# Hybrid decoder layer: the attention's keys and values prepared in the projection stage, and one reciprocal for the gates

## The chip, the core and the metric

One core of a Trainium2 chip runs the whole kernel. Its engines are TensorE (PE), VectorE (DVE), ScalarE (ACT), GpSimd (POOL) and SyncE (SP), each with its own instruction queue that it works off in order; SP only issues transfers here. The metric is the device time of one execution in microseconds; less is better.

## What is computed

A decoder layer on 1024 tokens of width 1024, in float32. One input projection feeds three parts: RWKV-7 time mixing (8 heads), a sparse attention with 8 query heads, 2 groups of keys and values and three branches (compressed, selected, sliding window), and two merge gates. Then come an output projection, cross-attention into 256 memory tokens, and a gated feed-forward net with a convolution. The change concerns the attention's keys and values and its gates:

```python
kv = p[..., NSA_DIM:NSA_DIM + 6 * NSA_KV_DIM].reshape(B, S, 6, G, dh)
k_c, v_c, k_s, v_s, k_w, v_w = [kv[:, :, i] for i in range(6)]
gates = jax.nn.sigmoid(p[..., NSA_DIM + 6 * NSA_KV_DIM:].reshape(B, S, Hq, 3))
q = partial_rope(q, pos)
k_c, k_s, k_w = partial_rope(k_c, pos), partial_rope(k_s, pos), partial_rope(k_w, pos)
...
s_s = jnp.einsum('bgrqd,bgqnkd->bgrqnk', qblk, ks)
p_s = jax.nn.softmax(s_s, axis=-1)
o_s = jnp.einsum('bgrqnk,bgqnkd->bgrqd', p_s, vs)
...
o = jnp.stack([o_c, o_s, o_w], axis=-1)
return jnp.einsum('bshdc,bshc->bshd', o, gates).reshape(B, S, NSA_DIM)
```

The rope turns the first 16 of the 64 numbers of each query and key by an angle that depends on the token.

## The kernel before

Every large float32 product is made of three matmuls in a reduced format (`mm3`, L194 to L197): each operand is split into a high part (a rounding copy, on ACT, L200) and a low part (the rest, a subtraction on VectorE, L201); this pair is `split`. Weights come in pieces by `wload` (L211): SP loads a piece into `raw` (L224; there are two such buffers), and `split` makes `wh` and `wl` of it (two buffers of each in each of two pools).

The program has a first stage (0 to about 210 us) with projections and everything that depends on them alone, the RWKV stage (to about 717 us), the attention stage, and then merge, output projection, cross-attention and feed-forward net. The order of each engine's instructions is fixed when the program is built.

`nsa_proj(cc, n, ...)` (L340) projects all 1024 tokens, in 8 tiles of 128, on n columns that belong to the sparse attention: 24 matmuls for each tile (`np`), an eviction to `nst` by ACT (L347), the rope of the key columns in place by POOL (L355 to L358, once for each z of nb blocks of columns; 128 tokens lie on the partitions), and a store of the tile to `rawn` in DRAM (L359). It is called with cc = 512 and 512 columns (compressed keys and values and the first pair of plain keys and values), with cc = 1024 and 280 columns (the second pair and the gates' 24 columns), and with cc = 0 (queries). The first two calls are called the first and the second projection here. In the first, the first four tiles are worked on together, so that they are complete after 96 matmuls; the other four follow one by one. Between the two lie the key and value projections of the memory (`mk`, `mv`) and transposes of the memory (`mT`); behind the second follow the compression of the keys (`cm`, on blocks `blkh` and `blkl` that are gathered from `rawn`), and more of `mk` and `mv`.

At the start of the attention stage the keys are read back from `rawn` (`kld`, POOL's queue), transposed by PE (`kT`, L985), and copied to `KHt` twice (each half of the partitions holds the high parts, L988, L989), with the low parts in `KL` (L990). The values are read back (`vld`) and split into `VV`. Gate matmuls (`gt`, the merge gates' projection) stand between these on PE. Then blocks of 128 queries follow: `queries(qb)` loads `qr` (L1009) and the gates `gr` (L1011), transposes the queries (`qT`, L1019), and the scores (`sc`, `st`), weights and values follow. `combined` divides by the sum of the weights, which is column 64 of the products, and multiplies by the gate.

Of the kernel before, what the change touches and what calls it, by code (L numbers as in the profile page):

```python
# [126 lines left out]
def layer_kernel(ctx: ExitStack, tc, I, out, cst):  # L127
# [3 lines left out]
    drp = ctx.enter_context(tc.tile_pool(name="drp", bufs=1, space=DRAM))  # L131
# [41 lines left out]
    def pst(name="pst"):  # L173
        return bank("t", name)
# [24 lines left out]
    def split(src, h, l):  # L199
        S.activation(h, src, AF.Copy)  # L200
        V.tensor_sub(l, src, h.bitcast(F32))  # L201
# [33 lines left out]
    def gemmN(o, act, tt, w, cc, n, nk=8):  # L235
        for k in range(nk):
            mm3(o, *act.sta(k, tt), *w.at(k, cc, n), k == 0, k == nk - 1)
# [15 lines left out]
    ps = pst("zz")  # L253
# [26 lines left out]
    wkv = W(2)  # L280
# [29 lines left out]
    for gi, grp in enumerate(groups):  # L310
        n = sum(r for _, r in grp)
        rows = p0.tile([P, P], F32, name=f"rows{gi}")
        o = 0
# [18 lines left out]
    yb = drp.tile([512, T], F32, name="yb")  # L332
    gscr = drp.tile([2048, T], F32, name="gscr")
    rawn = drp.tile([T, NSA_COLS], F32, name="rawn")


    cso = p0.tile([P, 2 * P], F32, name="cso")
    SP.dma_start(cso, cst[:, C_COS:C_CAU])

    def nsa_proj(cc, n, scale, nb, nh, w=None, ahead=lambda tt: None):  # L340
        w = w or wload([win[:, NSA0 + cc:NSA0 + cc + n]])
        for tt in range(NT):
            ahead(tt)
            ps = pg("np")
            gemmN(ps[:, :n], xT, tt, w, 0, n)
            t = stt([P, HALF], name="nst")
            S.activation(t[:, :n], ps[:, :n], AF.Copy, scale=scale)  # L347
            v = t[:, 0:256 * nb].rearrange("p (b h d) -> p b h d", h=4, d=64)[:, :, 0:nh, 0:16]
            for z in range(nb):
                vz = v[:, z]  # L350
                co = cso[:, tt * 16:tt * 16 + 16]
                si = cso[:, P + tt * 16:P + tt * 16 + 16]
                a = p0.tile([P, nh, 16], F32, name="rpa", tag="rpa", bufs=2)
                b = p0.tile([P, nh, 16], F32, name="rpb", tag="rpb", bufs=2)
                G.tensor_tensor(a, vz, bc(co, nh), op=OP.mult)  # L355
                G.tensor_tensor(b[:, :, 0:8], vz[:, :, 8:16], bc(si[:, 0:8], nh), op=OP.mult)
                G.tensor_tensor(b[:, :, 8:16], vz[:, :, 0:8], bc(si[:, 8:16], nh), op=OP.mult)
                G.tensor_tensor(vz, a, b, op=OP.add)  # L358
            SP.dma_start(rawn[tt * P:(tt + 1) * P, cc:cc + n], t[:, :n])  # L359

    rows_h = [slice(0, 64), slice(64, 128)]

# [109 lines left out]
            for u in range(2 * kh, 2 * kh + 2):  # L472
                wkv_split(u)

    nsa_proj(512, 512, 1.0, 2, 2, wkv, first)
    mem_load()
    for rows, pos, n in rowt:
        pt = pst("pv")
# [13 lines left out]
    mem_k(0)  # L492
    mem_v(0)
    blocks = windows(512, "nsa_pe_k")
    nsa_proj(1024, 280, 1.0, 1, 2)
    compress(*blocks, "nsa_ck_w1", "nsa_ck_w2", True)
    mem_k(1)
    blocks_v = windows(640, "nsa_pe_v")
# [451 lines left out]
    with tc.manual_schedule(engines={mybir.EngineType.PE}):  # L950
        while not all(t.done for t in outputs_):
            for tasks in classes:
                t = next((t for t in tasks if not t.done), None)
# [9 lines left out]
    n_scope, npl = opened("npl")  # L963
# [5 lines left out]
    flags = npl.tile([P, 4], F32, name="flags")  # L969
# [2 lines left out]


    gate_chunk(GT)
    KHs, VVs = [], []
    KL = npl.tile([67, 2, 2, T], F32R, name="KL")
    for br, cc in enumerate((768, 1024)):
        kl_ = b8([P, NT, P], name="kld")
        G.dma_start(kl_, rawn[:, cc:cc + P].rearrange("(a p) c -> p a c", p=P))
        KHt = npl.tile([P, 2, T], F32R, name=f"KHt{br}")  # L980
        V.tensor_copy(KL[64:67, br].rearrange("p g t -> p (g t)"), flags[64:67, 2 + br:3 + br].to_broadcast([3, 2 * T]))
        for j in range(2):
            ps = pst("kT")
            for i in range(4):
                PE.transpose(ps[:, i * P:(i + 1) * P], kl_[:, 4 * j + i, :], ident)  # L985
            sl = slice(j * HALF, (j + 1) * HALF)
            for g, rw in enumerate(rows_h):
                S.activation(KHt[rw, g, sl], ps[rw], AF.Copy)  # L988
                S.activation(KHt[rows_h[1 - g], g, sl], ps[rw], AF.Copy)  # L989
                V.tensor_sub(KL[0:64, br, g, sl], ps[rw], KHt[rw, g, sl].bitcast(F32))  # L990
        KHs.append(KHt)
        vl_ = b8([P, NT, 2, 64], name="vld")
        G.dma_start(vl_.rearrange("p a g d -> p a (g d)"), rawn[:, cc + P:cc + 2 * P].rearrange("(a p) c -> p a c", p=P))
        VV = npl.tile([P, NT, 2, 129], F32R, name=f"VV{br}")
        V.memset(VV[:, :, :, 64:65].bitcast(F32), 1.0)
        split(vl_, VV[:, :, :, 0:64], VV[:, :, :, 65:129])
        VVs.append(VV)

    for j in range(2):
        n = (C_ANY - C_CAU) // 2  # L1000
# [4 lines left out]
    def queries(qb):  # L1005
        qr = stt([P, 4, 2, 64], name="qr")
        src = rawn[qb * P:(qb + 1) * P, 0:512].rearrange("t (g r d) -> g t r d", g=2, r=4)
        for g in range(2):
            SP.dma_start(qr[:, :, g, :], src[g])  # L1009
        gr = sm.tile([P, 8, 3], F32, name="gr", tag="gr", bufs=3)  # L1010
        SP.dma_start(gr, rawn[qb * P:(qb + 1) * P, 1280:1304].rearrange("t (h c) -> t h c", c=3))  # L1011
        S.activation(gr, gr, AF.Exp, scale=-1.0)
        V.tensor_scalar(gr, gr, 1.0, None, op0=OP.add)
        V.reciprocal(gr, gr)
        if qb == 0:
            V.tensor_scalar(gr[:, :, 0], gr[:, :, 0], flags[:, 0:1], None, op0=OP.mult)
        ps = pst("qT").rearrange("p (r t) -> p r t", t=P)
        for r in range(4):
            PE.transpose(ps[:, r, :], qr[:, r].rearrange("p g d -> p (g d)"), ident)  # L1019
        Q = npl.tile([P, 8, P], F32R, tag="q", bufs=2, name="Q")  # L1020
        Q2 = b8([67, 2, 4, P], F32R, name="Q2")
        for g, rw in enumerate(rows_h):
            gs = slice(g * 4, g * 4 + 4)
            S.activation(Q[rw, gs, :], ps[rw], AF.Copy)
            V.tensor_sub(Q[rows_h[1 - g], gs, :], ps[rw], Q[rw, gs, :].bitcast(F32))
            S.activation(Q2[0:64, g], ps[rw], AF.Copy)
        return Q, Q2, gr
# [107 lines left out]
    def combined(qb, g, br, t, gr, O):  # L1135

        ps = pst("poT")[:, 0:260].rearrange("p (r n) -> p r n", n=65)
        for r in range(4):
            PE.transpose(ps[:, r, :], t[:, r * P:(r + 1) * P], ident[0:65, 0:65])
        rs = sm.tile([P, 4], F32, name="prs", tag="prs", bufs=4)  # L1140
        V.reciprocal(rs, ps[:, :, 64])
        V.tensor_tensor(rs, rs, gr[:, g * 4:g * 4 + 4, br], op=OP.mult)
        d = O[:, g * 4:g * 4 + 4, :]
        first = br == BRANCHES[0]
        o = d if first else npl.tile([P, 4, 64], F32, name="po2", tag="po2", bufs=2)
        V.tensor_tensor(o, ps[:, :, 0:64], rs[:, :, None].to_broadcast([P, 4, 64]), op=OP.mult)
        if not first:
            G.tensor_tensor(d, d, o, op=OP.add)
        if g == 1 and br == BRANCHES[-1]:
            late.append((LS, lambda: stored(qb, O)))  # L1150
# [103 lines left out]
    for i, (qb, g) in enumerate(items):  # L1254
# [4 lines left out]
        nb = sum(span(qb, br)[1] for br in BRANCHES)  # L1259
# [24 lines left out]
    w = dict(zip((2, 3), cur["wmb"]))  # L1284
# [20 lines left out]
    for j, k in todo:  # L1305
        g = gate_load(1, k, 0, lambda sh, name: stt(sh, name=name))
        ps = pg("mg")
# [117 lines left out]
    for h in range(XQ):  # L1425
        x_query(h)
        if h == 0:
            kvh = [b8([P, 2048], F32R, f"kvh{i}") for i in range(2)]
            kvl = [b8([P, 2048], F32R, f"kvl{i}") for i in range(2)]
            for i in range(2):  # L1430
                t = b8([P, 2048], name="kvld")
# [33 lines left out]
    f = 0  # L1465
    for n in (2, 4, 4, 4, 4, 4):
# [4 lines left out]
        for i in range(n):  # L1471
            w = wload([wup[:, (f + i) * P:(f + i + 1) * P], wup[:, FF + (f + i) * P:FF + (f + i + 1) * P]])
            gt = b8([P, 2, T], F32R, "gT")
            last = [sm.tile([P, 2], F32, name="cl", tag="cl", bufs=6) for _ in range(2)]
            for half in range(2):
                c = []
                for q in range(2):
                    ps = pg("up")
# [4 lines left out]
                hs = slice(half * HALF, (half + 1) * HALF)  # L1483
# [12 lines left out]
        if done:  # L1496
            w = [cols(0), cols(1)]
# [4 lines left out]
        else:  # L1502
            for j in range(2):
                w = cols(j)
# [30 lines left out]
```

## Time and profile before

| | |
|---|---|
| median of 3 runs | 2225.76 us (2222.63 to 2226.09) |
| the profiled execution | 2223.49 us, span 2221.7 us, mean granted PE clock 0.988 |
| PE busy | 2131.7 us, 96% of the span |
| VectorE, ACT, POOL busy | 55%, 40%, 21% |
| transfers | 157.91 MB |

The span is the time from the first to the last instruction that the profile shows; the profiled execution's own time is 1.8 us longer. Busy shares are means over stages with different limits.

### The profile page before, as it was taken

How to read it: one execution, taken by the hardware profiler on the slowest of the kernel's cores; microseconds unless marked ns; L12 is line 12 of the kernel's file. 1: busy time of each engine (PE TensorE's matmuls, PEld its weight loads, DVE VectorE, ACT ScalarE, POOL GpSimd, SP SyncE). 2: the span in 40 equal slices, each digit the busy share in tenths (PEclk: the TensorE clock that was granted, in tenths of full speed). 3: DMA queues.
4: the chain of work that ended last, by engine and by line, in shares of the span. 5: the costliest groups of instructions: out<-in, count | busy, mean ns of one | idle time of the engine just before them, and what ended most of it. 6: DMA issues, size and time to landing. Idle time of an engine off the chain costs nothing.

```text
span 2221.7 us, 31651 instructions
## 1 busy us (share of the span) xinstructions
PE 2131.7 (96%) x12301; PEld 1706.0 (77%) x12301; DVE 1232.4 (55%) x2416; ACT 889.2 (40%) x1441; POOL 475.0 (21%) x544
## 2 busy tenths in 40 slices
PE   9989999999999899999899999999999999999997
PEld 7978777777778667756678877788888888888886
DVE  3422576777652787888656535275444434344447
ACT  3433443544533576776523424142322313132232
POOL 2112231333300244444422101030100101000013
PEclk9999999999999999999999999999999999999999
DMA  6544112121223321112252313111111111111102
GB/s 206 152 150 124 49 24 56 36 52 32 62 59 94 110 66 45 42 45 68 72 189 86 123 38 114 39 39 57 38 48 48 54 42 57 39 57 57 57 29 86
DMA packets 196659, 157.91 MB, mean 71 GB/s; under 512 B 49061, under 2 KB 164766, under 8 KB 196510
## 3 DMA queue, kind: packets, MB, share of 16 engines
q1 hardware_dynamic: 184798, 139.10, 21.2%
q10 hardware_dynamic: 11136, 14.68, 2.0%
q0 software_dynamic: 576, 2.10, 0.3%
q8 instruction: 98, 1.61, 0.3%
q14 instruction: 51, 0.42, 0.1%
HBM read 125.86 MB, written 29.98 MB: 70 GB/s over the span
## 4 chain that ended last, share of the span: by engine, by line
PE 47%; DVE 5%; ACT 2%; DMA 1%; issue 1%; POOL 0%; SPq 0%; ACTq 0%; DVEq 0%; POOLq 0%
PE up L196 7%; PE up L197 7%; PE up L195 7%; PE dn L195 4%; PE dn L197 4%; PE dn L196 4%; PE op L195 2%; PE op L197 1%; PE op L196 1%; PE xq L195 1%; PE xq L196 1%; PE xq L197 1%; DVE acc L1334 1%; ACT acc L1333 1%; DVE bs L1327 1%
## 5 line engine op out<-in xcount | busy, mean ns | idle before, releaser
L200 ACT ACTIVATE wh<-raw 128x1024 fp32r<-128x1024 f32 (+1 forms) x160 | 168.8, 1055 | 474.9 <-PE dn L197 138.1
L201 DVE TENSOR_TENSOR wl<-raw,wh 128x1024 fp32r<-128x1024 f32 (+1 forms) x160 | 198.1, 1239 | 282.5 <-ACT wh L200 281.5
L196 PE MATMUL up<-nTl,wh 128*128 128x512 f32 x704 | 276.5, 393 | 0.0
L197 PE MATMUL up<-nTh,wl 128*128 128x512 f32 x704 | 276.4, 393 | 0.0
L195 PE MATMUL up<-nTh,wh 128*128 128x512 f32 x704 | 276.4, 393 | 0.0
L1458 DVE SCALAR_TENSOR_TENSOR cv<-up,pv,cv 128x511 f32<-128x511 f32 (+1 forms) x176 | 131.5, 747 | 145.4 <-ACT cv L1456 143.4
L1482 POOL TENSOR_TENSOR cv<-cv 128x512 f32<-128x512 f32 x44 | 56.8, 1291 | 630.9 <-DVE cl L1462 413.5
L196 PEld LDWEIGHTS up<-nTl,wh 128*128 128x128 f32 x704 | 132.3, 188 | 29.6
L195 PEld LDWEIGHTS up<-nTh,wh 128*128 128x128 f32 x704 | 132.2, 188 | 29.6
L197 PEld LDWEIGHTS up<-nTh,wl 128*128 128x128 f32 x704 | 132.2, 188 | 29.6
L1106 POOL TENSOR_TENSOR pl<-pe,ph 128x512 fp32r<-128x512 f32 x87 | 114.3, 1317 | 161.3 <-ACT ph L1105 97.3
L195 PE MATMUL dn<-wh,gT 128*128 128x512 f32 x352 | 138.1, 393 | 0.2 <-ACT wh L200 0.2
L197 PE MATMUL dn<-wh,gT 128*128 128x512 f32 x352 | 137.5, 391 | 0.0
L196 PE MATMUL dn<-wl,gT 128*128 128x512 f32 x352 | 136.9, 389 | 0.0
L1493 DVE SCALAR_TENSOR_TENSOR acc<-acc,dn 128x512 f32<-128x512 f32 x96 | 65.5, 686 | 95.5 <-PE dn L197 94.9
L1456 ACT ACTIVATE cv<-up,pv 128x512 f32<-128x512 f32 x88 | 68.5, 778 | 117.2 <-PE up L197 117.2
L195 PE MATMUL gt<-xTh,wh 128*128 128x512 f32 x256 | 113.0, 441 | 0.5 <-DVE nm L1074 0.5
L197 PE MATMUL gt<-xTh,wl 128*128 128x512 f32 x256 | 102.3, 399 | 0.0
L196 PE MATMUL gt<-xTl,wh 128*128 128x512 f32 x256 | 101.9, 398 | 0.0
L1335 POOL TENSOR_TENSOR acc<-acc,lngb 128x1024 f32<-128x1024 f32 x21 | 50.4, 2401 | 206.0 <-DVE acc L1334 129.8
L1105 ACT ACTIVATE ph<-pe 128x512 fp32r<-128x512 f32 (+1 forms) x148 | 90.2, 627 | 6.9 <-POOL macc L1223 4.6
L195 PE MATMUL prj<-xTh,wh 128*128 128x512 f32 x208 | 90.5, 435 | 2.2 <-ACT wh L200 2.2
(365 smaller groups left out, 5092.2 us busy)
## 6 DMA issues: line engine op xcount, KB each, us to landing
raw<-in_ffn_w_up_dram SPq DMA_DIRECT2D x88, 256.0 KB
raw<-in_w_in_dram SPq DMA_DIRECT2D x33, 512.0 KB
raw<-in_ffn_w_down_dram SPq DMA_DIRECT2D x22, 512.0 KB
gscr<-gst ACTq DMA_DIRECT2D x32, 256.0 KB
rawn<-nst SPq DMA_DIRECT2D x16, 256.0 KB
raw<-in_xa_wk_dram SPq DMA_DIRECT2D x8, 512.0 KB
raw<-in_xa_wv_dram SPq DMA_DIRECT2D x8, 512.0 KB
gl<-gscr SPq DMA_DIRECT2D x16, 256.0 KB
```

The costliest lines, as they stand in the source:

```text
L195: PE.matmul(o, lh, rh, start=start, stop=False)
L196: PE.matmul(o, lh, rl, start=False, stop=False)
L197: PE.matmul(o, ll, rh, start=False, stop=stop)
L200: S.activation(h, src, AF.Copy)
L201: V.tensor_sub(l, src, h.bitcast(F32))
L1105: S.activation(h, e, AF.Copy)
L1106: in_turn("l", LTURN)(l, e, h.bitcast(F32), op=OP.subtract)
L1335: (V if tt == NT - 1 else G).tensor_tensor(r[:, c], r[:, c], gb[:, 1, c], op=OP.add)
L1456: S.activation(c, ps, AF.Identity, scale=pc("cw2", ci), bias=pc("ffn_conv_b", ci))
L1458: V.scalar_tensor_tensor(c[:, s:], ps[:, :HALF - s], pc(nme, ci), c[:, s:], op0=OP.mult, op1=OP.add)
L1482: G.tensor_tensor(c[0], c[0], c[1], op=OP.mult)
L1493: V.scalar_tensor_tensor(v, v, 1.0 if f else ALPHA, ps, op0=OP.mult, op1=OP.add)
```

## The change

`nsa_proj` gets an argument `kv = (br, o, keep)` for the first two projections: br is the pair's number (0 or 1), o the first column of its 128 key columns in the tile, and keep the columns that are still stored to `rawn`. For each tile PE transposes the rotated key columns (L370 of the kernel after) into a bank that collects four tiles; after the fourth they are split (`kp`) and stored to DRAM, `KHd` and `KLd`. The value columns are split into `vt`, with a column of ones between, and stored to `VVd`. In the attention stage the transposes, copies, subtractions and value splits are gone; instead `KHt` is loaded from `KHd` by eight transfers of 256 KB, four issued by SP and four by POOL, and `KL` and `VV` by two transfers each on POOL's queue (512 KB and 1032 KB each). The sigmoid 1/(1 + exp(-x)) of a gate and the division by the sum of the weights were two reciprocals, multiplied; now the sum is multiplied by 1 + exp(-x), and one reciprocal is taken. The factor from `flags`, which is 0 for tokens without a compressed block, moves from the gate to that reciprocal.

```diff
-    def nsa_proj(cc, n, scale, nb, nh, w=None, ahead=lambda tt: None):
+    def nsa_proj(cc, n, scale, nb, nh, w=None, ahead=lambda tt: None, kv=None):
...
-            SP.dma_start(rawn[tt * P:(tt + 1) * P, cc:cc + n], t[:, :n])
+            if kv is None:
+                SP.dma_start(rawn[tt * P:(tt + 1) * P, cc:cc + n], t[:, :n])
+                continue
+            br, o, keep = kv
+            SP.dma_start(rawn[tt * P:(tt + 1) * P, cc + keep.start:cc + keep.stop], t[:, keep])
+
+            half, q = divmod(tt, 4)
+            if q == 0:
+                pk = pst("kT")
+            PE.transpose(pk[:, q * P:(q + 1) * P], t[:, o:o + P], ident)
+            if q == 3:
+                kh, kl = (p0.tile([P, HALF], F32R, name="kp", tag=f"kp{i}", bufs=1) for i in range(2))
+                split(pk, kh, kl)
+                hs = slice(half * HALF, (half + 1) * HALF)
+                SP.dma_start(KHd[br][:, hs], kh.bitcast(F32))
+                SP.dma_start(KLd[br][:, hs], kl.bitcast(F32))
+            v = t[:, o + P:o + 2 * P].rearrange("p (g d) -> p g d", g=2)
+            vt = p0.tile([P, 2, 129], F32R, name="vt", tag="vt", bufs=2)
+            V.memset(vt[:, :, 64:65].bitcast(F32), 1.0)
+            split(v, vt[:, :, 0:64], vt[:, :, 65:129])
+            SP.dma_start(VVd[br][tt * P:(tt + 1) * P, :], vt.rearrange("p g c -> p (g c)").bitcast(F32))
...
-    nsa_proj(512, 512, 1.0, 2, 2, wkv, first)
+    nsa_proj(512, 512, 1.0, 2, 2, wkv, first, kv=(0, 256, slice(0, 256)))
...
-    nsa_proj(1024, 280, 1.0, 1, 2)
+    nsa_proj(1024, 280, 1.0, 1, 2, kv=(1, 0, slice(256, 280)))
...
-    for br, cc in enumerate((768, 1024)):
-        kl_ = b8([P, NT, P], name="kld")
-        G.dma_start(kl_, rawn[:, cc:cc + P].rearrange("(a p) c -> p a c", p=P))
...
+    for g, gr_ in enumerate(rows_h):
+        for br in range(2):
+            for e, rw in zip((SP, G), rows_h):
+                e.dma_start(KHs[br][rw, g].bitcast(F32), KHd[br][gr_, :])
+    for br in range(2):
...
-        for j in range(2):
-            ps = pst("kT")
-            for i in range(4):
-                PE.transpose(ps[:, i * P:(i + 1) * P], kl_[:, 4 * j + i, :], ident)
-            sl = slice(j * HALF, (j + 1) * HALF)
-            for g, rw in enumerate(rows_h):
-                S.activation(KHt[rw, g, sl], ps[rw], AF.Copy)
-                S.activation(KHt[rows_h[1 - g], g, sl], ps[rw], AF.Copy)
-                V.tensor_sub(KL[0:64, br, g, sl], ps[rw], KHt[rw, g, sl].bitcast(F32))
...
-        split(vl_, VV[:, :, :, 0:64], VV[:, :, :, 65:129])
-        VVs.append(VV)
+        G.dma_start(KL[0:64, br].bitcast(F32), KLd[br].rearrange("(g d) t -> d g t", g=2))
+        G.dma_start(VVs[br].rearrange("p a g c -> p a (g c)").bitcast(F32), VVd[br].rearrange("(a p) c -> p a c", p=P))
...
-        V.reciprocal(gr, gr)
-        if qb == 0:
-            V.tensor_scalar(gr[:, :, 0], gr[:, :, 0], flags[:, 0:1], None, op0=OP.mult)
...
-        V.reciprocal(rs, ps[:, :, 64])
-        V.tensor_tensor(rs, rs, gr[:, g * 4:g * 4 + 4, br], op=OP.mult)
+        V.tensor_tensor(rs, ps[:, :, 64], gr[:, g * 4:g * 4 + 4, br], op=OP.mult)
+        V.reciprocal(rs, rs)
+        if qb == 0 and br == 0:
+            V.tensor_scalar(rs, rs, flags[:, 0:1], None, op0=OP.mult)
```

**Where the instructions stand.** PE in the first projection, at the end of its first four tiles (96 matmuls). Before, matmul follows matmul:

```order
L195 MATMUL np<-wh,xTh_93 128x512
L196 MATMUL np<-wl,xTh_93 128x512
L197 MATMUL np<-wh,xTl_95 128x512
L195 MATMUL np<-wh,xTh_96 128x512
L196 MATMUL np<-wl,xTh_96 128x512
L197 MATMUL np<-wh,xTl_98 128x512
```

After:

```order
L197 MATMUL np<-wh,xTl_95 128x512
L370 MATMUL kT<-ident,nst 128x128
L195 MATMUL np<-wh,xTh_96 128x512
L370 MATMUL kT<-ident,nst 128x128 x2
L196 MATMUL np<-wl,xTh_96 128x512
L197 MATMUL np<-wh,xTl_98 128x512
L195 MATMUL np<-wh,xTh_96 128x512
L370 MATMUL kT<-ident,nst 128x128
L196 MATMUL np<-wl,xTh_96 128x512
```

The transposes of tiles 0 to 3 stand behind matmuls 96, 97, 97 and 100. Those of tiles 4 to 6 stand five matmuls behind the end of their tile, that of tile 7 behind the end of the projection, three transposes of parameters and six of `mT`. In the second projection they stand behind matmuls 39 and 54, then every 24 (six behind the end of their tile), and the last one eight `cm` matmuls behind the end. Each waits for ACT and POOL.

SP at the start of the attention stage, before:

```order
L224 DMA raw<-in_w_in_dram 128x8x128
L970 DMA flags<-in_const_dram 128x4
L1009 DMA qr<-rawn 128x4x64 x4
L1167 DMA yld<-ya 128x512 x2
L1002 DMA csn<-in_const_dram 128x768 x2
```

After:

```order
L224 DMA raw<-in_w_in_dram 128x8x128
L992 DMA flags<-in_const_dram 128x4
L1003 DMA KHt_7636<-KHd_147 64x1024
L1003 DMA KHt_7637<-KHd_148 64x1024
L1003 DMA KHt_7636<-KHd_147 64x1024
L1003 DMA KHt_7637<-KHd_148 64x1024
L1012 DMA csn<-in_const_dram 128x768 x2
L1019 DMA qr<-rawn 128x4x64 x4
```

Four key loads and the two loads of `csn` (384 KB each) stand ahead of the four query loads. On PE there, 39 `gt` matmuls stood between the last step of the RWKV stage and the first eight `kT`, then 16 `gt`, eight `kT`, a `gt` and `qT`; now 73 `gt` stand there without a break, and then `qT`.

SP behind the second projection, after (before, the two loads at the ends followed each other with one store of `rawn` between):

```order
L224 DMA raw<-in_nsa_ck_w_dram 128x4x256
L365 DMA rawn<-nst 128x24
L375 DMA KHd_148<-kp 128x512
L376 DMA KLd_150<-kp 128x512
L381 DMA VVd_152<-vt 128x258
L224 DMA raw<-in_xa_wk_dram 128x4x256 x2
```

The stores of the last tile's keys and values stand ahead of the load of the next weights, `in_xa_wk`; a small load for the compression of the values (`w2s`), which stood between the two loads of `in_xa_wv`, stands ahead of both.

## Rows read from the trace of the kernel before

**Rows 1.** page, busy time, share and instructions of one engine
```profile
PE 2131.7 (96%) x12301; PEld 1706.0 (77%) x12301; DVE 1232.4 (55%) x2416; ACT 889.2 (40%) x1441; POOL 475.0 (21%) x544
```

**Rows 2.** windows: length, busy time of each engine, clock, DMA share, GB/s
```profile
70.00:96.00 26.00, 26.00 (x204) 25.90 (x203) 8.23 (x9) 8.79 (x14) 7.86 (x29) 1.00 0.46 132
96.00:120.00 24.00, 19.87 (x158) 18.27 (x158) 14.49 (x21) 12.80 (x19) 1.47 (x4) 1.00 0.60 180
120.00:140.00 20.00, 14.69 (x107) 12.73 (x106) 8.03 (x9) 9.05 (x15) 0.00 (x0) 1.00 0.56 171
140.00:180.00 40.00, 39.95 (x171) 31.52 (x170) 3.67 (x3) 7.41 (x11) 12.00 (x48) 1.00 0.29 95
715.00:730.00 15.00, 12.59 (x60) 10.10 (x58) 5.40 (x10) 5.52 (x9) 4.07 (x4) 1.00 0.85 230
730.00:745.00 15.00, 12.04 (x39) 8.50 (x40) 10.80 (x16) 11.98 (x19) 0.88 (x1) 0.77 0.45 138
```

**Rows 3.** timeline of PE, both projections: start, length, line, names
```profile
32.09 0.39 PE L197 MATMUL np<-wh,xTl 128*128 128x512 f32 x1
...
54.33 0.40 PE L197 MATMUL np<-wh,xTl 128*128 128x512 f32 x1
...
75.11 0.29 PE L197 MATMUL np<-wh,xTl 128*128 128x280 f32 x1
...
94.87 0.29 PE L197 MATMUL np<-wh,xTl 128*128 128x280 f32 x1
```

**Rows 4.** timeline of POOL, first projection, tiles 0 to 4
```profile
30.74 0.25 POOL L355 TENSOR_TENSOR rpa<-nst,cso 128x32 f32<-128x32 f32 x1 [30.29 <-DMA cso<-in_const_dram]
...
31.88 0.46 POOL L358 TENSOR_TENSOR nst<-rpa,rpb 128x32 f32<-128x32 f32 x2
...
36.56 0.46 POOL L358 TENSOR_TENSOR nst<-rpa,rpb 128x32 f32<-128x32 f32 x2
...
40.11 0.47 POOL L358 TENSOR_TENSOR nst<-rpa,rpb 128x32 f32<-128x32 f32 x2
```

**Rows 5.** timeline of ACT, both projections
```profile
38.23 0.60 ACT L347 ACTIVATE nst<-np 128x512 f32<-128x512 f32 x1 [5.10 <-PE np L197]
...
77.62 0.67 ACT L347 ACTIVATE nst<-np 128x280 f32<-128x280 f32 x2
...
82.85 0.40 ACT L347 ACTIVATE nst<-np 128x280 f32<-128x280 f32 x1 [2.70 <-PE np L197]
```

**Rows 6.** timeline of POOL, second projection
```profile
78.14 1.98 POOL L355 TENSOR_TENSOR rpa<-nst,cso 128x32 f32<-128x32 f32 x1 [20.86 <-ACT nst L347]
...
80.56 0.25 POOL L358 TENSOR_TENSOR nst<-rpa,rpb 128x32 f32<-128x32 f32 x1
...
84.02 0.26 POOL L358 TENSOR_TENSOR nst<-rpa,rpb 128x32 f32<-128x32 f32 x1
...
97.29 0.26 POOL L358 TENSOR_TENSOR nst<-rpa,rpb 128x32 f32<-128x32 f32 x1
```

**Rows 7.** timeline of DVE, second projection
```profile
77.75 2.26 DVE L201 TENSOR_TENSOR blkl<-blk,blkh 128x2016 fp32r<-128x2016 f32 x1 [0.55 <-ACT blkh L200]
```

**Rows 8.** timeline of PE, start of the attention stage
```profile
722.81 1.03 PE L985 MATMUL kT<-ident,kld 128*128 128x128 f32 x8
...
730.66 0.66 PE L985 MATMUL kT<-ident,kld 128*128 128x128 f32 x4 [3.08 <-DMA kld<-rawn]
```

**Rows 9.** timeline of SP's queue: issues of transfers
```profile
97.98 0.39 SPq L224 DMA_DIRECT2D raw<-in_xa_wk_dram  x1
...
720.95 4.50 SPq L1009 DMA_DIRECT2D qr<-rawn  x4
```

**Rows 10.** windows of 2 us, start of the attention stage
```profile
726.00:728.00 2.00, 1.58 (x7) 0.97 (x6) 1.45 (x2) 0.43 (x1) 0.00 (x0) 1.00 1.23 317
728.00:730.00 2.00, 0.00 (x0) 0.00 (x0) 1.97 (x3) 0.35 (x1) 0.00 (x0) 1.00 1.05 268
...
734.00:736.00 2.00, 2.00 (x6) 1.52 (x6) 1.48 (x3) 1.94 (x4) 0.00 (x0) 0.50 0.85 227
```

More of the change, by code (lines that the diff above doesn't have):

```diff
@@ L334, in layer_kernel @@
     rawn = drp.tile([T, NSA_COLS], F32, name="rawn")
+    KHd, KLd = ([drp.tile([P, T], F32, name=f"{n}{br}") for br in range(2)] for n in ("KHd", "KLd"))
+    VVd = [drp.tile([T, 258], F32, name=f"VVd{br}") for br in range(2)]
     cso = p0.tile([P, 2 * P], F32, name="cso")
     SP.dma_start(cso, cst[:, C_COS:C_CAU])
-    def nsa_proj(cc, n, scale, nb, nh, w=None, ahead=lambda tt: None):
+    def nsa_proj(cc, n, scale, nb, nh, w=None, ahead=lambda tt: None, kv=None):
         w = w or wload([win[:, NSA0 + cc:NSA0 + cc + n]])
@@ L974, in layer_kernel @@
     gate_chunk(GT)
-    KHs, VVs = [], []
     KL = npl.tile([67, 2, 2, T], F32R, name="KL")
-    for br, cc in enumerate((768, 1024)):
-        kl_ = b8([P, NT, P], name="kld")
-        G.dma_start(kl_, rawn[:, cc:cc + P].rearrange("(a p) c -> p a c", p=P))
-        KHt = npl.tile([P, 2, T], F32R, name=f"KHt{br}")
-        V.tensor_copy(KL[64:67, br].rearrange("p g t -> p (g t)"), flags[64:67, 2 + br:3 + br].to_broadcast([3, 2 * T]))
-        for j in range(2):
-            ps = pst("kT")
-            for i in range(4):
-                PE.transpose(ps[:, i * P:(i + 1) * P], kl_[:, 4 * j + i, :], ident)
-            sl = slice(j * HALF, (j + 1) * HALF)
-            for g, rw in enumerate(rows_h):
-                S.activation(KHt[rw, g, sl], ps[rw], AF.Copy)
-                S.activation(KHt[rows_h[1 - g], g, sl], ps[rw], AF.Copy)
-                V.tensor_sub(KL[0:64, br, g, sl], ps[rw], KHt[rw, g, sl].bitcast(F32))
[L991 to L995, printed above, removed]
-        split(vl_, VV[:, :, :, 0:64], VV[:, :, :, 65:129])
-        VVs.append(VV)
+    KHs = [npl.tile([P, 2, T], F32R, name=f"KHt{br}") for br in range(2)]
+    VVs = [npl.tile([P, NT, 2, 129], F32R, name=f"VV{br}") for br in range(2)]
+    for g, gr_ in enumerate(rows_h):
[3 more added lines that the diff above has]
+    for br in range(2):
+        V.tensor_copy(KL[64:67, br].rearrange("p g t -> p (g t)"), flags[64:67, 2 + br:3 + br].to_broadcast([3, 2 * T]))
+        G.dma_start(KL[0:64, br].bitcast(F32), KLd[br].rearrange("(g d) t -> d g t", g=2))
+        G.dma_start(VVs[br].rearrange("p a g c -> p a (g c)").bitcast(F32), VVd[br].rearrange("(a p) c -> p a c", p=P))
     for j in range(2):
```

## The prediction

> **What bounds the kernel now.** I read the page first: TensorE (PE) is busy for 2131.7 of 2221.7 us [rows 1], so it idles for 90 us in all, and whatever makes it wait anywhere lengthens the kernel unless one of those idle stretches takes it up. Next the windows over the stretches that the change touches [rows 2]: from 70 to 96 us, where the second of the two changed projections runs, PE does not idle at all; from 96 to 140 us it idles for 4.1 + 5.3 = 9.4 us, waiting for weights; from 140 us on it is full again; around 730 us, where the attention stage starts, it idles for 2.4 + 3.0 = 5.4 us in 30. Then the timelines of GpSimd (POOL), PE and ScalarE (ACT) in those stretches, for one question: when PE comes to a new transpose, are the keys ready? The keys are ready only when POOL has turned them (the rope, four operations for each group of heads), and PE, which takes its matmuls in the order written, can do nothing else while it waits.
>
> **First projection, 512 columns.** Matmuls 96 and 192 start at 32.09 and 54.33 us, so a matmul takes 22.24/96 = 0.232 us of PE [rows 3]. POOL has not begun when PE is half through: its first rope sat 30.29 us until the table of cosines came, and the last addition of tile 0 ends at 31.88 + 0.46 = 32.34, the fourth tile's at 36.56 + 0.46 = 37.02, one tile each 1.56 us [rows 4]. The order puts transpose 0 behind matmul 96 (PE is there at 32.33: wait 0.1), transpose 1 one matmul on (ready 33.9, PE there 32.7: 1.2), transpose 2 at once behind it (1.5), transpose 3 three matmuls, 0.7 us, on (1.56 - 0.7: 0.8). That is 3.6 us. Tiles 4 to 6 depend on ACT's eviction: it starts at 38.23 [rows 5], 0.57 behind the start of the tile's last matmul (32.09 + 24 x 0.232 = 37.66), and POOL ends at 40.11 + 0.47 = 40.58 [rows 4]. The transpose stands behind five matmuls of the next tile, so PE is there 6 x 0.232 = 1.39 us from 37.66, at 39.05: a wait of 1.5, three times, 4.6. For tile 7 nine small transposes stand in between instead of five wide matmuls; I take 1.2 (0.8 to 1.7 by the same subtraction). **Sum 9.4 us.** Bounds 5 (later tiles hit POOL at its quickest) to 10.5.
>
> **Second projection, 280 columns.** Matmuls 39 and 192 start at 75.11 and 94.87: 0.129 us each [rows 3]. ACT evicts tile 0 only at 77.62, behind a large split of the compression's windows [rows 5], and POOL's first multiplication then takes 1.98 us where the same one took 0.25 before [rows 4, 6], so the tile's rope ends at 80.56 + 0.25 = 80.81. Transpose 0 stands behind matmul 39, PE is there at 75.24: a wait of 5.6 us. Tiles 1 to 6: eviction at 82.85 (tile 3), rope done at 84.02 + 0.26 = 84.28; that tile's last matmul starts at 94.87 - 96 x 0.129 = 82.47, and the transpose stands seven slots on, at 83.37: 0.9 us, six times, 5.5. **Sum 11.1 us**, bounds 6 (the waits of the small tiles shrink because PE, once late, never gains on ACT and POOL) to 13. Tile 7 (rope done 97.29 + 0.26 = 97.55, PE there at about 96) belongs to the next term.
>
> The slow multiplication has a row beside it: VectorE's split of the windows runs from 77.75 to 80.01, and POOL's operation ends at 80.12 [rows 6, 7]. The Trainium skill (SBUF — State Buffer, section "SBUF: two separate sides") says that GpSimd and a VectorE operation with two SBUF inputs exclude each other for the length of an instruction. This row agrees. By that rule the 16 new value subtractions on VectorE, with two such inputs, would each hold up a rope by their own length, which I estimate from its rows at 0.25 us, up to 4 us in all; the sum here goes without it.
>
> **The transposes themselves.** Eight took 1.03 us [rows 8]; sixteen are added in stage 1: **2.1 us**. The same sixteen go from stage 3 (below). The new key and value splits are ACT's and VectorE's, whose cover is PE's 48 matmuls of a pair of tiles; they cost nothing there except through the queues below.
>
> **The chain of weight loads from 96 to 140 us.** There the loads set the pace: PE idles 9.4 us [rows 2]. SP issues the next weight load at 97.98 [rows 9]. In the new order three writes stand ahead of it, and the first waits for transpose 7 (97.55 at the earliest), ACT's and VectorE's halves of the split (0.6 each, as ACT's 128x512 eviction [rows 5]) and then three issues: near 100.5, against 97.98, and a small weight load now also stands ahead of the value weights. **Plus 3 us**, bounds 0 (the buffer wasn't free before) and 5. The chain starts from a buffer that the second projection's matmuls free, so I let the earlier 11 us pass whole.
>
> **The granted clock.** PE sat idle from 727.6 to 730.66; the clock was 1.00 until then, and 0.50 in 734:736 [rows 8, 10]; over 730:745 its mean is 0.77, so 15 x 0.23 = 3.4 us went [rows 2]. A 5.6 us idle (second projection) and a stretch with 3.6 of 5 us idle (first) are of that size, while 96:140 with its many short gaps stayed at 1.00 [rows 2]. One such loss nearly certain, the other half: **plus 3.5 us**, bounds 0 and 8.
>
> **Stage 3.** What goes: the idle of 5.4 us (3.08 of it for the old key load [rows 8]), the 3.4 us of slow clock and 2.1 us of transposes, about 11. The 16 copies, 8 subtractions and 2 value splits that also go are ACT's and VectorE's; they cost only through those idles. What comes: the query load. SP issued it at 720.95 [rows 9], right behind the flags. Now four key loads of 256 KB and two table loads of 384 KB stand ahead of it, 1.8 MB, and its own 0.5 MB; POOL's queue meanwhile carries 1.05 + 1.05 + 2.1 = 4.2 MB of keys and values. The DMA engines moved 268 to 317 GB/s when full [rows 10]. With all of that rate the 2.36 MB land 7.9 us on, at 729; with half of it (150 GB/s) 15.7 us on, at 736.7. PE reaches the query's transpose 34 gate matmuls after 722.81 [rows 8], by the same 0.232 us at 730.7. So it waits 0 to 6 us, near 4.5 with the issues and a weight load ahead; behind it stand score matmuls and the gate matmuls, all of them. Add 2 for the waits inside the first query block (part of the 5.4), 2.5 for the clock after such an idle, 0.9 for a PSUM bank: 10 against 11. **Minus 1 us**; bounds: no wait and no slow clock, minus 9; a wait of 8 with the losses on top, plus 5.
>
> The gate: eight reciprocals of a small tile go from VectorE, and one multiplication and one reciprocal change places; two tiny operations are added. VectorE is busy for 55% and PE does not wait there. Zero, within 1 either way. The rest of the attention stage is written in a slightly different order, within 2 either way.
>
> **The sum.** 9.4 + 11.1 + 2.1 + 3 + 3.5 - 1 = 28.1 us on the profiled execution's 2223.5: 2251.6. The median of the runs shown is 2.3 above it; I give 2253.
>
> **The rivals.**
> (B) Faster. At the start of stage 3 the query lands before PE wants it, and 9 us are won; and PE does not wait in stage 1, because the keys are there. Then 2223.5 + 2.1 - 9 = 2217. It decides once the stage-1 costs are under 9 us. Against it: the ends of the ropes [rows 4, 6] lie behind PE's slots in all tiles, in all but the first by 0.8 us or more.
> (C) Half hidden. The 9.4 us of idle between 96 and 140 take up the second projection's lateness, if the load chain there doesn't start later with it: 28.1 - 9.4 = 18.7, about 2243; with a better stage 3, 2235. For it: the chain's transfers are the limit there. Against: the buffers that they fill are freed by PE.
> (D) Stage 3 becomes a matter of transfers: 5.2 MB instead of 2.1, the query behind 1.8 MB of it. A wait of 8 us and its clock: plus 5 instead of minus 1, 2259. The Trainium skill (DMA: Bandwidth & Descriptors, "Issuing engines are not separate DMA queues") says that transfers issued by SP and GpSimd interleave on the same 16 engines, so that splitting the key loads over both saves issue time alone. By that rule the query lands with the even share, at 736.7, which is this case's cheaper half. The 268 to 317 GB/s with both queues busy agree.
> (E) The clock stays low for longer, 8 us instead of 3.5: 2258.
> (F) No effect: waits of stage 1 and gains of stage 3 cancel, 2221 to 2230.
>
> **Chances.** My case 0.52, C 0.20, D and E 0.17, B 0.06, F 0.05. Ends 2234 (C with a good stage 3) and 2268 (D, E and the port together). A measurement here tells about 0.2%, 4.5 us, from no change. Faster 0.06, same 0.05, slower 0.89.
>
> **What would show it.** In the profile after: PE's waits on POOL's rope near 20 us in 16 waits, the longest near 5.6 us at 75 to 81; slow clock behind it; the SP load at 97.98 some 15 to 25 us later; PE's first query transpose waiting for a DMA. Wrong if those waits are under 10 us in sum, if the second projection's delay is gone at 150 us, or if stage 3 begins without a wait and runs 9 us shorter.

## The result, and the profile after

The changed kernel takes 2256.61 us (median of 4 runs, 2254.26 to 2259.33) against 2225.93 us (2222.63 to 2227.1): a ratio of 1.0144, 95% interval 1.0131 to 1.0157. It is slower by 31 us; 2253 were forecast, with a range that holds the result. The sum was right, but two of its terms were not, and their errors have opposite signs: the first stage costs 21 us where 29 were forecast, and the attention stage costs 12 where it was to win 1.

From the page after, the span and the engines' row that answers to [rows 1]:

```profile
span 2252.4 us, 31773 instructions
...
PE 2137.8 (95%) x12301; PEld 1707.2 (76%) x12301; DVE 1224.1 (54%) x2433; ACT 885.0 (39%) x1443; POOL 477.8 (21%) x548
```

PE is busy for 6 us more and idles for 25 us more. What it waited for, over the whole span (engine, line, what released it: us in all, times, the longest):

```profile
PE kT L370 <- POOL nst L360: 16.5, 15, 2.4
PE gt L195 <- ACT gst L569: 13.2, 3, 11.8
...
PE qT L1026 <- DMA qr<-rawn: 2.1, 1, 2.1
```

The first row is new and stands where the prediction looked for it. The second, 11.8 us in one piece, is new and wasn't foreseen. Where the time went is read by following the same instruction through both traces. Three of ACT's serve as marks: its last eviction of the memory's keys (at 196.8 us before), the last eviction of `Y` at the end of the RWKV stage (714.9), and the sixteenth copy of a query block's maxima, `Q<-row`, at the end of the attention stage (1080.8). Delays against the kernel before, in us:

| kernel | at 196.8 | at 714.9 | at 1080.8 | within the attention stage |
|---|---|---|---|---|
| changed | +23.8 | +20.9 | +32.8 | +11.9 |
| `e1_new_first` | +25.3 | +25.8 | +24.9 | -0.9 |
| `e2_new_attention` | +6.1 | +10.8 | +21.8 | +11.1 |
| `e3_late` | +4.6 | +4.5 | +15.1 | +10.6 |
| `e4_loads_behind` | +26.9 | +24.1 | +20.6 | -3.5 |
| `e5_late_loads` | +5.8 | +3.7 | -4.4 | -8.0 |
| `e6_gate` | +1.5 | +5.3 | +6.2 | +0.9 |
| `e7_late_query_first` | +3.5 | +2.7 | -1.8 | -4.5 |
| `e8_large_rows` | +25.5 | +23.7 | +35.5 | +11.7 |

The last two marks of the kernel before:

```profile
714.85 0.82 ACT L901 ACTIVATE Y<-Y,pv 128x512 f32<-128x512 f32 x1 [2.33 <-DVE Y L900]
...
1080.80 0.59 ACT L1078 ACTIVATE Q<-row 3x512 fp32r<-3x512 f32 x1
```

And the last one of the changed kernel (the one before it, at 735.75, stands further down):

```profile
1113.59 0.59 ACT L1085 ACTIVATE Q<-row 3x512 fp32r<-3x512 f32 x1
```

Up to 714.9, `e6_gate` differs from the kernel before only by a few tiny reciprocals that it lacks, and still it is 5 us late there in its profiled execution, while its timed runs show no difference; so single entries are good to about 5 us, and verdicts rest on the timed runs.

**First stage.** PE's timeline, the new transposes (start, length, line, names; in brackets the idle time ahead and what ended it), tiles 4 and 5 of the first projection, tiles 0, 1 and 7 of the second:

```profile
43.77 0.33 PE L370 MATMUL kT<-ident,nst 128*128 128x128 f32 x1 [1.36 <-POOL nst L360]
...
51.03 0.33 PE L370 MATMUL kT<-ident,nst 128*128 128x128 f32 x1 [1.36 <-POOL nst L360]
...
89.24 0.33 PE L370 MATMUL kT<-ident,nst 128*128 128x128 f32 x1 [2.36 <-POOL nst L360]
...
92.29 0.33 PE L370 MATMUL kT<-ident,nst 128*128 128x128 f32 x1 [0.80 <-POOL nst L360]
...
118.70 0.33 PE L370 MATMUL kT<-ident,nst 128*128 128x128 f32 x1 [1.52 <-POOL nst L360]
```

And POOL's last addition of tile 4's rope, which answers to the last of [rows 4]:

```profile
43.26 0.45 POOL L360 TENSOR_TENSOR nst<-rpa,rpb 128x32 f32<-128x32 f32 x2
```

And ACT's eviction of the second projection's tile 0, which answers to the middle row of [rows 5]:

```profile
85.95 0.38 ACT L349 ACTIVATE nst<-np 128x280 f32<-128x280 f32 x1
```

The first projection's rope ends at 43.26 + 0.45 = 43.71, and PE takes the transpose 0.06 us later. From one transpose to the next PE needs 7.26 us; 24 matmuls take 5.56 [rows 3]. Of the 1.70 us between them 1.36 are idle, and the other 0.34 are not all the transpose's. `e3_late` (below) has the same transposes at places where they don't wait:

```profile
43.96 0.27 PE L354 MATMUL kT<-ident,nst 128*128 128x128 f32 x1
...
49.64 0.27 PE L354 MATMUL kT<-ident,nst 128*128 128x128 f32 x1
```

There 5.68 us lie between two of them, 0.12 more than 24 matmuls take. So a transpose costs 0.12 us, and a wait 0.22 more than its idle time. Most of that is overlap lost: a matmul's row lasts 0.39 us and the next one starts 0.23 behind its start, so 0.16 overlap, but nothing overlaps the last matmul in front of an idle.

**Attention stage.** PE, ACT, SP's issues and POOL's issues at its start:

```profile
749.90 0.39 PE L197 MATMUL gt<-xTh,wl 128*128 128x512 f32 x1
762.07 0.80 PE L195 MATMUL gt<-xTh,wh 128*128 128x512 f32 x1 [11.78 <-ACT gst L569]
...
768.83 1.08 PE L1026 MATMUL qT<-ident,qr 128*128 128x128 f32 x4 [2.12 <-DMA qr<-rawn]
```

```profile
735.75 0.81 ACT L923 ACTIVATE Y<-Y,pv 128x512 f32<-128x512 f32 x1 [2.32 <-DVE Y L922]
...
760.47 1.06 ACT L200 ACTIVATE wh<-raw 128x1024 fp32r<-128x1024 f32 x1 [15.97 <-DMA raw<-in_w_in_dram]
761.43 0.58 ACT L569 ACTIVATE gst<-gt 128x512 f32<-128x512 f32 x1
```

```profile
740.59 0.37 SPq L224 DMA_DIRECT2D raw<-in_w_in_dram  x1
...
742.39 7.08 SPq L1003 DMA_DIRECT2D KHt<-KHd  x4
749.57 11.17 SPq L1012 DMA_DIRECT2D csn<-in_const_dram  x2
760.78 3.83 SPq L1019 DMA_DIRECT2D qr<-rawn  x4
```

```profile
737.86 2.30 POOL L1003 DMA_DIRECT2D KHt<-KHd  x4
```

The reader is to see a chain over three engines. A load of gate weights is issued at 740.59, and POOL issues its eight key and value loads from 737.86 on. The weights land at 760.5 (ACT's split `wh<-raw` waited 15.97 us for this transfer), 20 us after the issue. ACT works in order, and the eviction `gst` of gate matmuls that PE had long finished stands behind that split; PE needs the bank that it empties. So PE stands still from 750.3 to 762.1 for a load whose weights it doesn't even need yet. Only then comes the query, 2.1 us. What the queues moved in 750 to 754 us (queue, kind: packets, MB, share of 16 engines; q0 is POOL's queue, q1 SP's, q10 ACT's):

```profile
q0 software_dynamic: 245, 0.94, 79.8%
q10 hardware_dynamic: 120, 0.21, 14.6%
q1 hardware_dynamic: 238, 0.12, 12.6%
```

POOL's queue and SP's queue moved about as many packets, 245 and 238. But POOL's were of 3.8 KB, and SP's, rows of 128 weights, of 512 bytes: 0.94 MB against 0.12. Ahead of that stands a stretch in which SP's queue moved nothing, although the load was issued at 740.59. In 741 to 745 us only two queues have packets:

```profile
q0 software_dynamic: 235, 0.76, 79.9%
q10 hardware_dynamic: 134, 0.25, 21.7%
```

So more than 4 of the 20 us passed before the load's first packet; why, no run shows.

What the stage costs in all, from the mark at 714.9 to that at 1080.8 (columns as in [rows 2]), before and after:

```profile
714.85:1080.80 365.95, 346.05 (x1671) 245.51 (x1670) 294.26 (x602) 250.31 (x437) 156.36 (x131) 0.99 0.22 63
```

```profile
735.75:1113.59 377.84, 349.30 (x1655) 246.87 (x1654) 278.31 (x584) 238.52 (x419) 158.12 (x135) 0.96 0.24 70
```

PE idles for 19.9 us before and 28.5 after, 8.6 more, and is busy for 3.3 us more with sixteen transposes less.

The clock (columns as in [rows 2]), behind the first projection's transposes, in the chain of weight loads, and behind PE's long idle:

```profile
68.00:70.00 2.00, 2.00 (x11) 2.00 (x11) 1.71 (x2) 1.91 (x3) 0.00 (x0) 0.50 0.70 197
70.00:72.00 2.00, 2.00 (x14) 2.00 (x14) 1.83 (x3) 0.09 (x1) 0.00 (x0) 0.67 0.65 155
...
150.00:152.00 2.00, 1.17 (x4) 0.58 (x3) 1.04 (x1) 0.93 (x1) 0.00 (x0) 0.50 0.72 244
...
772.00:774.00 2.00, 2.00 (x7) 1.52 (x6) 0.64 (x1) 0.48 (x1) 0.00 (x0) 0.50 0.01 2
```

It stood at half for about 3.5 us at 68 to 72, again at 150 to 157, and from 754 to 774; in the last 12 us of that PE works, and a gate matmul's row lasts 0.63 us instead of 0.39.

### The profile page after: what moved, and what is told of

Its sections match the earlier page's. It is cut to its first block, busy times and chain, and to the rows that moved or that the text cites. A ratio compares the mean times of both kernels' runs of the same rounds, so it can differ in the third digit from the quotient of the medians.

```text
span 2252.4 us, 31773 instructions
## 1 busy us (share of the span) xinstructions
PE 2137.8 (95%) x12301; PEld 1707.2 (76%) x12301; DVE 1224.1 (54%) x2433; ACT 885.0 (39%) x1443; POOL 477.8 (21%) x548
## 3 DMA queue, kind: packets, MB, share of 16 engines
q8 instruction: 98, 1.61, 0.3%
## 4 chain that ended last, share of the span: by engine, by line
PE 46%; DVE 5%; ACT 2%; issue 1%; DMA 1%; POOL 0%; SPq 0%; ACTq 0%; DVEq 0%; POOLq 0%
PE up L197 7%; PE up L196 7%; PE up L195 7%; PE dn L195 4%; PE dn L197 4%; PE dn L196 4%; PE op L195 1%; PE op L196 1%; PE op L197 1%; PE xq L195 1%; PE xq L196 1%; PE xq L197 1%; DVE acc L1343 1%; ACT acc L1342 1%; DVE bs L1336 1%
```

## The experiments

The time of the kernel before is that of the runs on the same chip; each ratio is against it, with its 95% interval.

**`e1_new_first`: the first stage alone.** The tile is stored whole, and the attention stage's old reading, transposing and splitting stands again.

```diff
-    nsa_proj(512, 512, 1.0, 2, 2, wkv, first, kv=(0, 256, slice(0, 256)))
+    nsa_proj(512, 512, 1.0, 2, 2, wkv, first, kv=(0, 256, slice(0, 512)))
-    nsa_proj(1024, 280, 1.0, 1, 2, kv=(1, 0, slice(256, 280)))
+    nsa_proj(1024, 280, 1.0, 1, 2, kv=(1, 0, slice(0, 280)))
```

> The projections as changed (transposes, splits and stores in the first stage), but the whole tile still stored, and the attention stage as before (keys read back, transposed and split there); only the gates' division is the new one. Theory A (two separate costs: about 21 us in the first stage from transposes that wait for GpSimd, about 10 us at the start of the attention stage from a starved weight load): first query transpose 20 to 23 us later than before, in all plus 21, about 2247 us. Rival B (the attention stage's 10 us come from the first stage's lateness or its other order, not from its own loads): plus 30, about 2256 us. Rival C (the attention stage's cost is larger and the first stage's delay is taken up later): under 2240 us.

Measured: 2245.27 us, ratio 1.0102 (1.0084 to 1.0119), so plus 21 to 23. PE's waits in it:

```profile
PE kT L370 <- POOL nst L360: 17.1, 15, 3.4
...
PE kT L1007 <- DMA kld<-rawn: 3.0, 1, 3.0
```

The waits for the ropes are those of the changed kernel, and at the start of the attention stage stands the old wait of 3 us for the keys, as in [rows 8]. In the profile the delay at the start of the attention stage is 26 us, where 20 to 23 were expected. Theory A holds for the first stage; B and C fall.

**`e2_new_attention`: the attention stage alone.** Stores from constant tiles take the place of transposes and splits.

```diff
-            PE.transpose(pk[:, q * P:(q + 1) * P], t[:, o:o + P], ident)
...
-                split(pk, kh, kl)
...
-                SP.dma_start(KHd[br][:, hs], kh.bitcast(F32))
+                SP.dma_start(KHd[br][:, hs], zz.bitcast(F32))
```

> The attention stage as changed, and the first stage without transposes and splits: the same transfers to the key and value arrays are issued at the same places, from constant tiles, so the attention works on constant keys and values. Theory A: nothing is lost in the first stage (start of the attention stage within 1.5 us of before), and about 10 us at its start, where the gate matmuls wait some 12 us for a weight load: about 2236 us. Rival B: the attention stage alone gains or costs nothing, 2215 to 2228 us. Rival C (the added stores, not the transposes, delay the first stage): start of the attention stage 10 us or more later, about 2245 us or more.

Measured: 2243.86 us, ratio 1.0086 (1.0068 to 1.0105). The number is the one that rival C gave, and theory A's missed it by 8 us. The trace divides it: 11.1 us fall in the attention stage, as A said, with the same wait as in the changed kernel:

```profile
PE gt L195 <- ACT gst L562: 12.3, 3, 10.8
```

The other 10.8 stand ahead of it, where A expected none: 6.1 by 196.8 us and 4.7 in the RWKV stage. Only 1.9 of them are more idle time of PE, in spite of four new waits for the second projection's weights at 70 to 77 us (3.3 us); 8.9 are more busy time, 3.7 of that in the RWKV stage, whose instructions are those of the kernel before, at a mean clock of 0.97 instead of 0.98. C's reading, that the added stores as such delay the first stage, doesn't hold either, since `e3_late` issues as many stores at nearly the same places and is 4.5 us late there. The timed runs have these 9 us too, so this part stays open.

**`e3_late`: the transposes one tile later.** They are owed, and paid behind a later tile's matmuls.

```diff
+            owed_k.append((max(tt + 1, 4 - br), tt, t))
...
             gemmN(ps[:, :n], xT, tt, w, 0, n)
+            keys(tt)
...
     mem_T()
+    last_k(NT)
```

> As the changed kernel, but each transpose of keys stands a whole tile of matmuls later (the first four of the first projection and the first three of the second together behind the fourth or fifth tile, the last ones behind the memory transposes and the first compression). Theory A: the waits for GpSimd (16.5 us in the changed kernel) fall to under 2 us, the transposes themselves stay (16 of about 0.2 to 0.33 us), so 14 to 18 us less than the changed kernel, about 2240 us; the attention stage still loses 10. Rival C (splits, stores and the chain of weight loads set the first stage's pace): the waits move to the weight loads, 2250 us or more. Rival D (the second projection's waits were hidden by idle behind it): only the first projection's 8 us come back, about 2248 us.

Measured: 2236.62 us, ratio 1.0058 (1.0042 to 1.0073): 19 to 20 us less than the changed kernel, a little more than the 14 to 18 expected: 16.5 us of idle and 0.22 for each of 15 waits make 19.8. The two longest sums of waiting on PE up to 220 us are the old ones for weights; no transpose waits for POOL any more:

```profile
PE cm L196 <- DVE wl L201: 3.0, 4, 0.9
PE cm L195 <- ACT wh L200: 2.3, 3, 1.0
```

The first stage's delay falls from 21 to 4.5 us at 714.9, with every transpose, split and store still in it. So the waits were the cost, with the restart behind each, and C and D fall. The attention stage keeps its loss of 10.6, with the same row on ACT:

```profile
743.40 1.06 ACT L200 ACTIVATE wh<-raw 128x1024 fp32r<-128x1024 f32 x1 [15.26 <-DMA raw<-in_w_in_dram]
```

**`e4_loads_behind`: the key and value loads on SP, behind the first queries.**

```diff
-            for e, rw in zip((SP, G), rows_h):
-                e.dma_start(KHs[br][rw, g].bitcast(F32), KHd[br][gr_, :])
...
+    def kv_load():
+        for br in range(2):
+            for g, gr_ in enumerate(rows_h):
+                for rw in rows_h:
+                    SP.dma_start(KHs[br][rw, g].bitcast(F32), KHd[br][gr_, :])
...
     qs = {NT - 1: queries(NT - 1)}
+    kv_load()
```

> As the changed kernel, but all key and value loads of the attention stage are issued by SP, behind the first query block's loads, and none by GpSimd. Theory A (the gate weights' load of 512-byte packets shares the transfer engines packet by packet with GpSimd's queue, whose packets are some 3.7 KB): the weight load lands within 5 us, its 11.8 us of waiting goes, and the query's wait with it; what remains is a wait for keys of 0 to 5 us: 6 to 11 us less than the changed kernel, 2246 to 2250 us. Rival E (the bytes are the limit): PE waits as long for the keys as it did for the weights, 2255 us or more.

Measured: 2238.21 us, ratio 1.0063 (1.0044 to 1.0081): 18 us less than the changed kernel, more than A's 6 to 11. The 11.8 us are gone, and PE's waits of over 1 us from 748 to 784 are two:

```profile
753.84 1.09 PE L1029 MATMUL qT<-ident,qr 128*128 128x128 f32 x4 [3.07 <-DMA qr<-rawn]
...
769.97 0.50 PE L195 MATMUL gt<-xTh,wh 128*128 128x512 f32 x1 [1.95 <-ACT gst L569]
```

The same bytes, in one queue and in the order of use, turn a loss of 11.9 us in this stage into a gain of 3.5. Rival E, that the bytes are the limit, falls. The run changes two things at once, the queue and the order; loads left to POOL but issued later weren't tried.

**`e8_large_rows`: the starved load with large packets.** Everything as in the changed kernel, but the last gate weights are read as 128 rows of 4 KB (from wrong columns).

```diff
-                SP.dma_start(raw[:, :, o:o + m], p[k0 * P:(k0 + ku) * P].rearrange("(k p) n -> p k n", p=P))
...
+                    SP.dma_start(raw.rearrange("p k n -> p (k n)"), whole)
...
+            if c == 15:
+                return c, wload([win[:, col0:col0 + P]], whole=win[0:P, 0:8 * P])
```

> As the changed kernel, but the last gate weights' load (512 KB) is read as 128 rows of 4 KB instead of 1024 rows of 512 bytes, from another part of the same weights, so that 128 columns of a gate are computed from wrong weights. Every other transfer stands as in the changed kernel. Theory A (the two queues take turns packet by packet): 128 packets are through after some 0.5 MB of GpSimd's queue, the load lands within 7 us instead of 20, the gate matmuls don't wait for it; the query, whose 2048 packets of 256 bytes stay as they are, is then what PE waits for, some 5 us earlier than now: 4 to 9 us less than the changed kernel, 2247 to 2252 us. Rival E (the bytes are the limit, or the order of issue): the load lands near 20 us as before, 2255 us or more.

Measured: 2256.02 us, ratio 1.0135 (1.012 to 1.0151): no gain, where A expected 4 to 9. The queues from 750 to 754, SP's issues, ACT's split and PE:

```profile
q0 software_dynamic: 173, 0.65, 55.2%
q1 hardware_dynamic: 171, 0.37, 36.4%
```

```profile
743.43 0.34 SPq L227 DMA_DIRECT2D raw<-in_w_in_dram  x1
...
756.78 11.47 SPq L1024 DMA_DIRECT2D qr<-rawn  x4
```

```profile
754.25 1.06 ACT L200 ACTIVATE wh<-raw 128x1024 fp32r<-128x1024 f32 x1 [6.89 <-DMA raw<-in_w_in_dram]
```

```profile
757.20 0.80 PE L195 MATMUL gt<-xTh,wh 128*128 128x512 f32 x1 [4.06 <-ACT gst L574]
...
772.38 1.09 PE L1031 MATMUL qT<-ident,qr 128*128 128x128 f32 x4 [10.54 <-DMA qr<-rawn]
```

The packets again go one for one, 173 and 171, and SP now moves 0.37 MB instead of 0.12. The load lands 10.8 us after its issue instead of 19.9, later than the 7 expected, and PE's wait for the eviction falls from 11.8 to 4.1 us. But the query, which stands behind keys and tables in the same queue, then keeps PE waiting for 10.5 us instead of 2.1: 14.6 here, 13.9 in the changed kernel. The load's first packet again comes late: in 743.5 to 747.5 us SP's queue moves none and POOL's 238. So the turns by packets are shown, but they are not the whole delay, and A's price was wrong: the weight load was the first of several transfers that all stood beside POOL's 4.2 MB. What costs is that queue's place beside the others, not the size of one load's rows.

**`e6_gate`: the gates' change alone**, on the kernel before.

> The kernel before with the gates' change alone (the sum multiplied by 1 + exp(-x), one reciprocal). Theory A: VectorE's work there hides beside TensorE, no difference: within 2.5 us of the kernel before. Rival: the reciprocal that now stands last lengthens each combination, 48 times about 0.1 us, plus 3 to 5 us.

Measured: 2225.27 us, ratio 0.9999 (0.9988 to 1.0009). No difference; the rival falls.

**`e5_late_loads`: both cures** (the edits of `e3_late` and `e4_loads_behind`).

> Both cures together: transposes one tile later, and the attention's key and value loads on SP behind the first queries. Theory A: costs of separate places add up, first stage plus 4.5 us over the kernel before, attention stage minus 3.4: within 3 us of the kernel before, 2222 to 2229 us. Rival: they are not independent, because the attention stage's gain needs a first stage that is late: 2232 us or more.

Measured: 2220.03 us, ratio 0.9971 (0.996 to 0.9982). It beats both kernels: about 6 us under the kernel before, about 37 under the changed one. That is 2 us below A's 2222 to 2229, since the attention stage gains 8.0 in the profile where 3.4 were expected; the rival falls. PE's waits from 705 to 750:

```profile
727.33 0.50 PE L195 MATMUL gt<-xTh,wh 128*128 128x512 f32 x1 [0.69 <-ACT gst L582]
...
732.08 0.63 PE L1042 MATMUL qT<-ident,qr 128*128 128x128 f32 x4 [1.74 <-DMA qr<-rawn]
...
736.79 0.50 PE L1086 MATMUL sc<-KHt,Q 128*128 128x512 f32 x1 [0.61 <-DVE part L1094]
...
745.53 0.50 PE L195 MATMUL gt<-xTh,wh 128*128 128x512 f32 x1 [0.61 <-ACT gst L582]
```

3.7 us in four, where the kernel before idled for 5.4 in 715 to 745 [rows 2]; the clock stays at 1.00.

**`e7_late_query_first`: both cures, and the first queries ahead of the mask tables.**

```diff
+    def kv_load():
+        key_load(0)
+        for j in range(2):
...
+            SP.dma_start(csn, cst[:, C_CAU + j * n:C_CAU + (j + 1) * n])
...
+        low_load(0)
+        key_load(1)
+        low_load(1)
```

> As the kernel with both cures, but the first block's queries are issued by SP ahead of the mask tables, then the keys of the first group, the tables, and the rest in the order of use. Theory A: the query's transpose waited 3.1 us behind the tables' 786 KB; that wait and its slow clock go, 3 to 5 us less than with both cures: 2218 to 2225 us, at or a little under the kernel before. Rival: the wait moves to the keys or tables (the transfers are the limit from 744 to 768 us): within 2 us of the kernel with both cures.

Measured: 2220.34 us, ratio 0.9979 (0.9967 to 0.9991), as `e5_late_loads`. The query's wait falls to 1.1 us, and other waits of 0.8 and 1.8 us for gate evictions come in. A's 2218 to 2225 holds the time, but its gain of 3 to 5 us over both cures isn't there. The rival had it.

## Why the prediction was right in sum and wrong in parts

**The first projection (9.4 us).** Right in kind and in size: waits of 0.55, 1.37, 0.53, three of 1.36 and 1.19, 7.7 us of idle, and with 0.22 for each of the seven about 9.3. The transposes came when the rope ended, as worked out.

**The second projection (11.1 us).** Mis-sized: 2.4 for tile 0 and six of 0.8, 7.3 us of idle and 8.8 with the restarts, and 1.5 for tile 7. Tiles 1 to 6 are within 0.1 of the 0.9. Tile 0's 5.6 was the error: PE comes 11.5 us later (matmul 39 starts at 86.59), ACT's eviction of that tile only 8.3 (85.95 against 77.62 [rows 5]), since it stands behind the split of the windows, which ends later than PE's tile. A late engine meets a less late partner, and that part of the wait is used up. The bound of 6 named such shrinking for the small tiles instead.

**The transposes (2.1 us).** Right: 0.12 each in `e3_late`, 2 for sixteen. The restart behind each wait, 0.22 us and 3.3 for all 15, is within the waits that the prediction worked out, since it subtracted start times.

**The aside on value subtractions (up to 4 us, also in the range's upper end).** Nothing of the kind shows: with the subtraction beside it, from 42.31 us, tile 4's rope took 1.63 us (42.08 to 43.71), and without it, in the kernel before, 1.61 (38.97 to 40.58).

**Load chain and clock (3 + 3.5 us).** From ACT's eviction of the second projection's tile 7 (+21.1) to 196.8 the delay grows by 2.7, tile 7's wait of 1.5 among it, where 3 and part of the clock's 3.5 were forecast. SP's load that had stood at 97.98 comes at 121.28, 2.2 us later than PE's lateness alone would put it, near the 2.5 worked out. Half clock came at 68 to 72, behind the first projection, not behind the wait of 2.4 us at 89 us, and in the load chain, which had kept 1.00 before; about 5 us of full clock went, partly in time that waits for weights anyway. One profile can't size this term: `e4_loads_behind`, with the same first stage, lost 10 in it. That rival C's idle would take up the delay is refuted by the same rows.

The first stage in sum: 29.1 forecast, 24 measured at 196.8 and 21 at the end of the RWKV stage.

**The attention stage (minus 1 us).** The failed step: "The DMA engines moved 268 to 317 GB/s when full", and from it that half of the rate would go to SP's queue, so that "it waits 0 to 6 us" for the query. Nearly as many packets went there as to POOL's, but these were small: in 742 to 758 us POOL's queue moved 987 packets and 3.7 MB, SP's 771 and 0.4 MB. The Trainium skill (DMA: Bandwidth & Descriptors, "Queues, rings and completion order") says that each DMA engine takes turns among the queues it has work for, a whole packet at a time. The counts of 245 and 238, and 173 and 171, agree; that SP's queue moved none in 741 to 745 us doesn't follow from it. So the gate weights, which the prediction counted among what stands ahead of the query and not as something PE waits for, came 20 us after their issue, and the in-order ACT carried this to PE. At the start of the stage idle went from 5.4 to 14.6 us (0.7 + 11.8 + 2.1), and some 5 us went to the clock instead of 3.4. Over the whole stage 8.6 of the 11.9 us are idle time and 3.3 busy time, although transposes were saved; 3.4 us went to half clock at 1095 to 1103, late in the stage, where the kernel before kept 1.00, and no term of the sum was for that. Rival D named the transfers, at 2259, but with bytes as the measure and the query as the victim.

**The gates (0 us).** Right (`e6_gate`).

**The rivals.** B's gain in the attention stage does exist once the loads have another place: 8 us in `e5_late_loads`, against its 9. It needed the first-stage cost under 9, and there it is 4 to 6.

## What to carry to other kernels

An operation that is moved ahead to where its data is made must be put behind the slowest helper of that data: here the same sixteen transposes cost 21 us right behind the rope and 4.5 a tile later. Before a load is put on a second queue, ask which small-row loads of the first queue are then in flight, and who stands behind them on an in-order engine: here it paid to put the largest transfers behind those that are needed first, in the same queue. And a sum that comes out right proves no term: that this one did was luck. Following a few instructions through both traces showed two errors of opposite sign, 8 us too much and 13 too little.

## What was not expected of the hardware

Two queues shared the engines one packet to one packet, whatever the sizes: 512 KB in rows of 512 bytes took 20 us beside a queue of 3.8 KB packets, and 10.8 us in rows of 4 KB, in both cases with more than 4 us ahead of the first packet. In `e4_loads_behind`, where POOL's queue is empty, the same load's 1024 packets were through within 4 us of its issue. The granted clock did not fall behind a single idle of 2.4 us in the second projection; it fell to 0.50 at 150 to 157 us after a row of idles of up to 1.0 us, where the kernel before had kept 1.00 with waits of up to 1.6 us. But `e6_gate`, whose first stage is nearly that of the kernel before, fell to 0.57 there too, at 128 to 132 us. What decides that was not tried.
